# Five buffers and other rates for background loads, and recurrence levels two ahead, in a hybrid layer

## The chip, the cores and the metric

The kernel runs on one core of a Trainium2 chip. The metric is the device time of one execution in microseconds (us), as the median of several runs. PE is TensorE (matmul), PEld its weight load, DVE is VectorE, ACT is ScalarE, POOL is GpSimd, and SP is the queue that issues DMAs.

## The reference

One layer over 256 latent and 256 context tokens of width 2048, in float32: a modulation from the conditioning vector c, a normalization, one wide input projection that feeds differential attention (8 heads) and a gated linear recurrence in both directions (8 heads), a merge of both by sigmoid gates, an output projection, and a gated MLP with a convolution of width 3.

```python
mod = jax.nn.silu(c) @ w_mod[l] + b_mod[l]          # 2048 -> 6 * 2048
h = modulate(x, norm1_w, sh1, sc1)
ak, av, rff, rfb, ri, aq, rq, rg, gate_a, gate_r = split_cols(h @ w_in, len(IN_SPLITS))
a = p[:, :, 0] - lam * p[:, :, 1]                   # attention: two softmaxes a head
rec = rec_readout(o_f + o_b, rg, rec_gnorm_w)       # rms_norm(o) * silu(rg)
y = jax.nn.sigmoid(gate_a) * (att @ w_branch_attn) + jax.nn.sigmoid(gate_r) * (rec @ w_branch_rec)
x = x + g1 * (y @ w_out)
x = x + g2 * conv_ffn(modulate(x, norm2_w, sh2, sc2), w_up, conv_w, conv_b, w_down)
```

The first third of `mod` is needed at once. The other two thirds, 64 tiles of w_mod (g1, sh2, sc2, g2), are needed only behind the merge.

## The kernel before

**Weight units.** All weights come from HBM in units of 512 KB (128 x 1024, float32). `stage` issues the DMA of a unit on SP into `raw` (4 buffers, L68). ACT casts it to its high part `whi` (L72), DVE subtracts that to get the low part `wlo` (L73; 3 buffers each), and PE multiplies with both: in the three-pass `gemm` (L77 to L79, projections that need the context tokens too) 24 matmuls a unit, in `gemm2` (L136, L137) 16 matmuls, in pairs.

**Order.** A tile scheduler puts the instructions in an order of its own on every engine, from the program order, priorities (the cast and the subtraction of `stage` are raised) and the number of buffers behind each tag. After each unit the program calls `tick`, which may start a background unit and lets generators run on: the attention's `head` (scores with S at L432, the reduction at L435, exponentials at L439, transposes of the probabilities tp at L451) and the recurrence's `head` (KQ at L565, transposes tp and ktp at L597 and L604, products of levels lv at L629 that are copied into S at L632, the output op at L637 to L640). A `yield n` waits for n ticks.

**Stages.** Statistics and first modulation (to some 145 us), attention (to 418), recurrence (to 745), readout (the eight RG tiles, then the normalization rrstd at L712 and the products rec; to some 797), merge (16 tiles y, L743 to L769; to 1045), output projection, FFN.

**Background units.** The 64 late tiles of w_mod are computed on DVE in 128 units, first half 0 of all tiles, then half 1: a DMA of 512 KB (L382), and some ticks later (`age`) one multiplication with the broadcast SiLU of c, `cb[half]`, that also sums along the row (L93). `bg_rate` sets how many are started per tick. A unit that was loaded waits in `held`. In attention and merge the buffers are those of the tag x1 (4), of which the two halves `cb` hold two; in the recurrence the heads' outputs `rraw` hold the other two, and units use the weight units' own `raw` buffers. Ahead of the recurrence's heads, `background(max(0, len(bg) - 64))` starts in a burst what is left of half 0.

Of the kernel before, what the change touches and what calls it, by code (L numbers as in the profile page):

```python
# [8 lines left out]
F32 = mybir.dt.float32  # L9
F32R = mybir.dt.float32r  # L10
U32 = mybir.dt.uint32
AF = mybir.ActivationFunctionType
ALU = mybir.AluOpType
# [3 lines left out]
P = 128  # L17
D = 2048
T = 256
# [6 lines left out]
NB = 10  # L26
C1 = 3
BG_ATT0 = 0.5
BG_ATT, BG_REC, BG_MRG = 0.7, 0.1, 0.6
# [12 lines left out]
def body(ctx, tc, cst_d, sel_d, cb_d, ccol_d, wn_d, xT_d, xc_d, lam_d, rope_d, mask_d, wm_d, wg0_d, win_d, wba_d,  # L42
         wbr_d, wout_d, wu0_d, wup_d, wdn_d, out_d):
    nc = tc.nc
    act, dve, pool, pe, dma = nc.scalar, nc.vector, nc.gpsimd, nc.tensor, nc.sync

    cpool = ctx.enter_context(tc.tile_pool(name="cpool", bufs=1))
    stg = ctx.enter_context(tc.tile_pool(name="stg", bufs=1))
# [38 lines left out]
    held, age = [], [2]  # L87

    def background_end(least=0):

        while held and held[0][0] >= least:
            _, raw, c_, dst = held.pop(0)
            dve.scalar_tensor_tensor(raw, raw, 1.0, c_, op0=ALU.mult, op1=ALU.mult, accum_out=dst)  # L93
# [69 lines left out]
    xpair = [big.tile([P, 2, 512], F32, tag="x1", name=f"xp{i}", bufs=4) for i in range(4)]  # L163
# [3 lines left out]
    with ExitStack() as es:  # L167
# [156 lines left out]
        for i in range(7):  # L324
            r = big.tile([P, 512], F32, tag="ar", name=f"g0sb{i}", bufs=16)
            if i % 2:
                dve.tensor_copy(r, g0[i])
            else:
                act.copy(r, g0[i])
            g0raw[GROUP0[i]] = r  # L330

        cb = [big.tile([P, 1024], F32, tag="x1", name=f"cb{i}", bufs=4) for i in range(2)]
        sg = big.tile([P, 1024], F32, tag="x1", name="sg", bufs=4)
        for i in range(2):
            dma.dma_start(cb[i], cb_d[:, i * 1024:(i + 1) * 1024])
            tc.keep_in_program_order(act.activation(sg, cb[i], AF.Sigmoid))
            tc.keep_in_program_order(dve.tensor_mul(cb[i], cb[i], sg))
# [30 lines left out]
    with ExitStack() as esa:  # L368
        bg_rate[0] = BG_ATT


        lane = [True]

        def background(n):
            for _ in range(n):
                if bg:
                    t, half = bg.pop(0)
                    if lane[0]:
                        raw = big.tile([P, 1024], F32, tag="x1", name="bgraw", bufs=4)
                    else:  # L380
                        raw = stg.tile([P, 1024], F32, tag="raw", name="raw", bufs=4)
                    dma.dma_start(raw, wm_d[t - 32, half])  # L382
                    held.append([0, raw, cb[half], modp[:, t - 32, half:half + 1]])
# [4 lines left out]
        with ExitStack() as es:  # L388
# [6 lines left out]
            lj = at.tile([P, 64], F32, name="lj")  # L395
            lamt = at.tile([P, 256], F32, name="lamt")
            dma.dma_start(lamt, lam_d)
# [20 lines left out]
            def head(h, kT, vr, qT):  # L418
# [61 lines left out]
                rs = at.tile([P, 2, T], F32, tag="rs", name="rs")  # L480
                act.activation(rs[:, 0], ops[:, 1], AF.Sqrt, bias=epst, scale=1.0 / P)
                dve.reciprocal(rs[:, 1], rs[:, 0])
                dve.scalar_tensor_tensor(o, o, subw, rs[:, 1], op0=ALU.mult, op1=ALU.mult)
# [40 lines left out]
        lane[0], age[0] = False, 8  # L524
        rraw = [big.tile([P, 4, T], F32, tag="x1", name=f"rraw{i}", bufs=4) for i in range(2)]
        rrstd = cpool.tile([P, T], F32, name="rrstd")
        with ExitStack() as es:
# [29 lines left out]
            def head(h, kkq, kc, PL, PC, vr):  # L557
# [43 lines left out]
                yield 2 if h in (0, 1, 7) else 1  # L601
# [5 lines left out]
                E = level(0)  # L607
# [15 lines left out]

                for li in range(7):
                    En = level(li + 1) if li < 6 else None
                    yield 1
                    lvp = rps.tile([P, 2, P], F32, tag="lv", name="lv", bufs=3)
                    for m in range(2):
                        pe.matmul(lvp[:, m], E[:, 0, m * P:(m + 1) * P], E[:, 1, m * P:(m + 1) * P],  # L629
                                  start=True, stop=True)  # L630
                    for m in range(2):
                        dve.copy_predicated(out=S4[:, 3 * m], mask=masks[:, li].bitcast(U32), data=lvp[:, m])  # L632
                    E = En
# [18 lines left out]
            background(max(0, len(bg) - 64))  # L652
            background_end()
            g01 = big.tile([P, 2, 2, T], F32, tag="x1", name="g01", bufs=4)
            depth[0] = 1
            bg_rate[0] = BG_REC
            for h in range(8):
                PL, PC = PLs[h % 2], PCs[h % 2]
# [37 lines left out]

            rg8 = rt.tile([P, 9, T], F32, tag="f", name="rgs")
            rgs = [rg8[:, 4 * i:4 * i + 4] for i in range(2)]
            for h in range(8):
                ps = in_tile(RG + h)  # L700
                s = rgs[h // 4][:, h % 4]
                t_ = rt.tile([P, T], F32, tag="rg", name="rg")
                fold(t_, ps)
                act.activation(s, t_, AF.Sigmoid)
                pool.tensor_tensor(s, t_, s, ALU.mult)
# [24 lines left out]
    def residual_load(i):  # L730
        t_ = big.tile([P, 4, T], F32, tag="x1", name=f"x1_{i}", bufs=4)
        dma.dma_start(t_, xT_d[:, 4 * i:4 * i + 4])
        x1.append(t_)
# [6 lines left out]
    lane[0], age[0] = True, 3  # L740
    bg_rate[0] = BG_MRG
    y = []
    for j in range(KT):  # L743
        if j == 4:
            residual_load(0)
# [108 lines left out]
    for j in range(FT):  # L854
        cs = []
        for s in range(2):
# [19 lines left out]
            u = et.tile([P, T], F32, tag=f"u{s}", name="u", bufs=2)  # L876
# [136 lines left out]
```

## Time and profile before

| | |
|---|---|
| median of three runs | 1888.81 us |
| the three runs | 1888.81, 1885.11, 1890.86 us |
| profiled execution, its time | 1883.4 us |
| its span | 1881.6 us |
| mean granted clock of PE, share of full speed | 0.995 |

The profiled execution lasts 1.8 us longer than its span, and is within the spread of measurements a little shorter than the three runs. Busy shares are averages over stages of different kinds, so stretches are looked at one by one.

### The profile page before, as it was taken

How to read it: one execution, taken by the hardware profiler on the slowest of the kernel's cores; microseconds unless marked ns; L12 is line 12 of the kernel's file. 1: busy time of each engine (PE TensorE's matmuls, PEld its weight loads, DVE VectorE, ACT ScalarE, POOL GpSimd, SP SyncE). 2: the span in 40 equal slices, each digit the busy share in tenths (PEclk: the TensorE clock that was granted, in tenths of full speed). 3: DMA queues.
4: the chain of work that ended last, by engine and by line, in shares of the span. 5: the costliest groups of instructions: out<-in, count | busy, mean ns of one | idle time of the engine just before them, and what ended most of it. 6: DMA issues, size and time to landing. Idle time of an engine off the chain costs nothing.

```text
span 1881.6 us, 27926 instructions
## 1 busy us (share of the span) xinstructions
PE 1833.5 (97%) x10416; PEld 1558.2 (83%) x10416; DVE 1353.2 (72%) x2131; ACT 997.2 (53%) x1507; POOL 382.1 (20%) x328
## 2 busy tenths in 40 slices
PE   7999999999999999999999999999999999999997
PEld 4777777887788888888888889888888888888886
DVE  4449989779866667988886779776777677654444
ACT  4336444557655556744455557555555555534342
POOL 0002111103223333411111111222222222211111
PEclk9999999999999999999999999999999999999998
DMA  9977777474233333688997665666656666666664
GB/s 387 369 266 256 229 230 238 142 239 137 93 113 112 102 103 122 211 302 305 321 321 249 190 191 179 192 190 190 191 190 191 190 191 190 182 194 187 193 188 132
DMA packets 108711, 385.69 MB, mean 205 GB/s; under 512 B 12320, under 2 KB 12448, under 8 KB 108576
## 3 DMA queue, kind: packets, MB, share of 16 engines
q1 hardware_dynamic: 108576, 383.92, 63.1%
q8 instruction: 81, 1.33, 0.3%
q14 instruction: 54, 0.44, 0.1%
HBM read 381.78 MB, written 2.10 MB: 204 GB/s over the span
## 4 chain that ended last, share of the span: by engine, by line
PE 78%; DVE 11%; DMA 6%; issue 3%; ACT 2%; POOL 0%; SPq 0%; DVEq 0%; ACTq 0%; POOLq 0%
PE macc L136 30%; PE macc L137 15%; PE acc L136 6%; DMA bgraw<-in_wm 5%; PE acc L77 5%; PE acc L79 5%; PE acc L78 5%; DVE wlo L73 3%; PE acc L137 3%; PE g L187 2%; DVE bgraw L93 2%; PE acc L187 2%; PE nat L187 2%; PE lv L629 1%; ACT whi L72 1%
## 5 line engine op out<-in xcount | busy, mean ns | idle before, releaser
L73 DVE TENSOR_TENSOR wlo<-raw,whi 128x1024 fp32r<-128x1024 f32 (+1 forms) x514 | 628.6, 1224 | 240.0 <-ACT whi L72 234.7
L72 ACT CAST whi<-raw 128x1024 fp32r<-128x1024 f32 (+1 forms) x514 | 530.9, 1034 | 422.1 <-PE macc L136 159.2
L136 PE MATMUL macc<-h,whi 128*128 128x512 f32 x1344 | 466.0, 391 | 0.0
L137 PE MATMUL macc<-h,wlo 128*128 128x256 f32 x1344 | 376.3, 280 | 0.0
L136 PE MATMUL acc<-h,whi 128*128 128x512 f32 x896 | 320.9, 400 | 0.0
L136 PEld LDWEIGHTS macc<-h,whi 128*128 128x128 f32 x1344 | 251.3, 187 | 55.1
L137 PEld LDWEIGHTS macc<-h,wlo 128*128 128x128 f32 x1344 | 254.0, 189 | 0.0
L137 PE MATMUL acc<-h,wlo 128*128 128x256 f32 x896 | 252.5, 282 | 1.2 <-DVE wlo L73 1.0
L136 PE MATMUL macc<-f,whi 128*128 128x512 f32 x704 | 244.1, 391 | 0.0
L77 PE MATMUL acc<-h,whi 128*128 128x512 f32 x528 | 212.1, 402 | 0.0
L79 PE MATMUL acc<-h,wlo 128*128 128x512 f32 x528 | 207.3, 393 | 0.3 <-DVE wlo L73 0.3
L78 PE MATMUL acc<-h,whi 128*128 128x512 f32 x528 | 206.4, 391 | 0.0
L136 PEld LDWEIGHTS acc<-h,whi 128*128 128x128 f32 x896 | 168.4, 188 | 37.7 <-issue 0.4
L137 PE MATMUL macc<-f,wlo 128*128 128x256 f32 x704 | 197.1, 280 | 0.0
L137 PEld LDWEIGHTS acc<-h,wlo 128*128 128x128 f32 x896 | 169.3, 189 | 4.9 <-DVE wlo L73 4.3
L93 DVE SCALAR_TENSOR_TENSOR bgraw<-bgraw,cb 128x1024 f32<-128x1024 f32 x105 | 133.0, 1268 | 36.8 <-DMA bgraw<-in_wm 36.0
L136 PEld LDWEIGHTS macc<-f,whi 128*128 128x128 f32 x704 | 131.6, 187 | 28.9
L884 POOL TENSOR_TENSOR u<-u 128x256 f32<-128x256 f32 x44 | 69.2, 1572 | 326.5 <-DVE u L879 286.5
L137 PEld LDWEIGHTS macc<-f,wlo 128*128 128x128 f32 x704 | 133.1, 189 | 0.0
L77 PEld LDWEIGHTS acc<-h,whi 128*128 128x128 f32 x528 | 99.2, 188 | 22.8 <-issue 4.3
L79 PEld LDWEIGHTS acc<-h,wlo 128*128 128x128 f32 x528 | 99.1, 188 | 22.6 <-DVE wlo L73 0.8
L78 PEld LDWEIGHTS acc<-h,whi 128*128 128x128 f32 x528 | 99.3, 188 | 19.2 <-issue 0.4
(752 smaller groups left out, 2674.4 us busy)
## 6 DMA issues: line engine op xcount, KB each, us to landing
raw<-in_win SPq DMA_DIRECT2D x178, 512.0 KB, 4.3
raw<-in_wup SPq DMA_DIRECT2D x168, 512.0 KB, 3.6
bgraw<-in_wm SPq DMA_DIRECT2D x105, 512.0 KB, 4.7
raw<-in_wdn SPq DMA_DIRECT2D x80, 512.0 KB, 3.6
nraw<-in_wn SPq DMA_DIRECT2D x64, 512.0 KB, 7.5
raw<-in_wout SPq DMA_DIRECT2D x32, 512.0 KB, 3.5
raw<-in_wm SPq DMA_DIRECT2D x23, 512.0 KB, 3.6
raw<-in_wba SPq DMA_DIRECT2D x16, 512.0 KB, 4.7
```

Of the source, the lines that this page charges most:

```text
L72: act.copy(hi[:, :n], raw[:, :n])
L73: dve.tensor_sub(lo[:, :n], raw[:, :n], hi[:, :n].bitcast(F32))
L77: pe.matmul(ps, wh, xh, start=first, stop=False)
L78: pe.matmul(ps, wh, xl, start=False, stop=False)
L79: pe.matmul(ps, wl, xh, start=False, stop=last)
L93: dve.scalar_tensor_tensor(raw, raw, 1.0, c_, op0=ALU.mult, op1=ALU.mult, accum_out=dst)
L136: pe.matmul(ps, hi[:, c_], xs[k][:, :, :T], start=k == 0, stop=False)
L137: pe.matmul(ps[:, :T], lo[:, c_], xs[k][:, 0, :T], start=False, stop=k == len(xs) - 1)
L187: tc.keep_in_program_order(pe.matmul(*args, **kw))
L629: pe.matmul(lvp[:, m], E[:, 0, m * P:(m + 1) * P], E[:, 1, m * P:(m + 1) * P], start=True, stop=True)
L884: pool.tensor_tensor(cs[1], cs[0], cs[1], ALU.mult)
```

## The change

There are five x1 buffers for four (one natural-layout buffer fewer, NB, and small tiles that share tags). Only half 0 of `cb` is prepared ahead of the attention; half 1 is loaded and multiplied by its sigmoid just before the readout. A unit of half 1 can't start before that. Rates and ages are new in all three stages: .5/.7 to .55/.77 in the attention, .1 to .05 in the recurrence, .6 to .74 in the merge; ages 2, 8 and 3 become 4, 3 and 5. The burst moves from ahead of the recurrence's heads to behind them, and all units use x1 buffers. In the recurrence's heads, head 0 and head 1 wait one and two ticks longer ahead of ktp, and levels E are made two ahead of their use instead of one. The residual's first load comes two tiles of y later, and the FFN's two tiles u become one.

```diff
-NB = 10
+NB = 9
-BG_ATT0 = 0.5
-BG_ATT, BG_REC, BG_MRG = 0.7, 0.1, 0.6
+BG_ATT0 = 0.55
+BG_ATT, BG_REC, BG_MRG = 0.77, 0.05, 0.74
+AGE_ATT, AGE_REC, AGE_MRG = 4, 3, 5
...
-    xpair = [big.tile([P, 2, 512], F32, tag="x1", name=f"xp{i}", bufs=4) for i in range(4)]
+    xpair = [big.tile([P, 2, 512], F32, tag="x1", name=f"xp{i}", bufs=5) for i in range(4)]
...
-        cb = [big.tile([P, 1024], F32, tag="x1", name=f"cb{i}", bufs=4) for i in range(2)]
-        sg = big.tile([P, 1024], F32, tag="x1", name="sg", bufs=4)
-        for i in range(2):
-            dma.dma_start(cb[i], cb_d[:, i * 1024:(i + 1) * 1024])
-            tc.keep_in_program_order(act.activation(sg, cb[i], AF.Sigmoid))
-            tc.keep_in_program_order(dve.tensor_mul(cb[i], cb[i], sg))
+        cb = {}
+
+        def cond(half, sg):
+
+            part = cb[half] = big.tile([P, 1024], F32, tag="x1", name=f"cb{half}", bufs=5)
+            dma.dma_start(part, cb_d[:, half * 1024:(half + 1) * 1024])
+
+            def rest():
+                tc.keep_in_program_order(act.activation(sg, part, AF.Sigmoid))
+                tc.keep_in_program_order(dve.tensor_mul(part, part, sg))
+            return rest
+
+        cond(0, big.tile([P, 1024], F32, tag="x1", name="sg", bufs=5))()
...
-                    t, half = bg.pop(0)
-                    if lane[0]:
-                        raw = big.tile([P, 1024], F32, tag="x1", name="bgraw", bufs=4)
-                    else:
-                        raw = stg.tile([P, 1024], F32, tag="raw", name="raw", bufs=4)
+                    t, half = bg[0]
+                    if half not in cb:
+                        return
+                    bg.pop(0)
+                    raw = big.tile([P, 1024], F32, tag="x1", name="bgraw", bufs=5)
                     dma.dma_start(raw, wm_d[t - 32, half])
-                    held.append([0, raw, cb[half], modp[:, t - 32, half:half + 1]])
+                    held.append([0, operation(raw, t, half)])
...
-        lane[0], age[0] = False, 8
-        rraw = [big.tile([P, 4, T], F32, tag="x1", name=f"rraw{i}", bufs=4) for i in range(2)]
+        age[0] = AGE_REC
+        rraw = []
...
-                yield 2 if h in (0, 1, 7) else 1
+                yield {0: 3, 1: 4, 7: 2}.get(h, 1)
...
-                E = level(0)
+                Es = [level(0)]
...
+                Es.append(level(1))
                 for li in range(7):
-                    En = level(li + 1) if li < 6 else None
+                    if li < 5:
+                        Es.append(level(li + 2))
                     yield 1
+                    E = Es.pop(0)
...
-                    E = En
...
-            background(max(0, len(bg) - 64))
-            background_end()
...
             for h in range(8):
+                if h % 4 == 0:
+                    rraw.append(big.tile([P, 4, T], F32, tag="x1", name=f"rraw{h}", bufs=5))
...
+            background(max(0, len(bg) - 64))
+            background_end()
+            held.append([0, cond(1, stg.tile([P, 1024], F32, tag="raw", name="sg", bufs=4))])
+
             rg8 = rt.tile([P, 9, T], F32, tag="f", name="rgs")
...
-    lane[0], age[0] = True, 3
+    age[0] = AGE_MRG
...
-        if j == 4:
+        if j == 6:
             residual_load(0)
...
+        us = et.tile([P, 2, T], F32, tag="gate", name="u", bufs=3)
...
-            u = et.tile([P, T], F32, tag=f"u{s}", name="u", bufs=2)
+            u = us[:, s]
```

How the change moves instructions is seen in the order of each engine, at three places.

On DVE, in the attention, in front of the eleventh reduction of scores (L435 before, L442 after); rows with modp are background operations (L93 before, L378 after). Before:

```order
L153 TENSOR_TENSOR qr<-qr,acc 128x256
L93 SCALAR_TENSOR_TENSOR bgraw,modp<-bgraw,cb_1243 128x1024
L412 STREAM_SHUFFLE rot<-qr 128x256
L93 SCALAR_TENSOR_TENSOR bgraw,modp<-bgraw,cb_1243 128x1024
L73 TENSOR_TENSOR wlo<-raw,whi 128x1024
L416 TENSOR_TENSOR qr<-t_2663,rot 128x256
L93 SCALAR_TENSOR_TENSOR bgraw,modp<-bgraw,cb_1243 128x1024
L514 TENSOR_TENSOR qT<-qr,qT 128x256
L93 SCALAR_TENSOR_TENSOR bgraw,modp<-bgraw,cb_1243 128x1024 x2
L73 TENSOR_TENSOR wlo<-raw,whi 128x1024
L482 RECIPROCAL rs<-rs 128x256
L435 TENSOR_REDUCE z<-S 128x2
```

and with the change:

```order
L461 TENSOR_TENSOR aT<-tp,aT 128x4x128
L153 TENSOR_TENSOR qr<-qr,acc 128x256
L378 SCALAR_TENSOR_TENSOR bgraw,modp<-bgraw,cb_1244 128x1024
L419 STREAM_SHUFFLE rot<-qr 128x256
L378 SCALAR_TENSOR_TENSOR bgraw,modp<-bgraw,cb_1244 128x1024
L423 TENSOR_TENSOR qr<-t_2667,rot 128x256
L74 TENSOR_TENSOR wlo<-raw,whi 128x1024
L521 TENSOR_TENSOR qT<-qr,qT 128x256
L378 SCALAR_TENSOR_TENSOR bgraw,modp<-bgraw,cb_1244 128x1024 x5
L74 TENSOR_TENSOR wlo<-raw,whi 128x1024
L489 RECIPROCAL rs<-rs 128x256
L442 TENSOR_REDUCE z<-S 128x2
```

Five background operations stood in the rows in front of the reduction, now there are seven, five of them in a row. Two subtractions wlo, on which PE's next units depend, stand among them in both orders.

On DVE, in the readout, around KQ of the last recurrence head (L565 before, L572 after); L716 and L729 are the readout's products. Before:

```order
L591 TENSOR_TENSOR E<-E,kkq 128x2x128
L93 SCALAR_TENSOR_TENSOR raw,modp<-raw,cb_1244 128x1024
L716 SCALAR_TENSOR_TENSOR rgs<-rraw_3599,cst,rgs 128x256
L73 TENSOR_TENSOR wlo<-raw,whi 128x1024 x2
L565 TENSOR_TENSOR KQ<-KQ,kc 128x512
L153 TENSOR_TENSOR rg<-rg,acc 128x256
L73 TENSOR_TENSOR wlo<-raw,whi 128x1024
L716 SCALAR_TENSOR_TENSOR rgs<-rraw_3599,cst,rgs 128x256
L586 TENSOR_TENSOR E<-PL_3625 128x256
L73 TENSOR_TENSOR wlo<-raw,whi 128x1024
```

and with the change:

```order
L729 SCALAR_TENSOR_TENSOR rgs<-rraw_3641,cst,rgs 128x256
L74 TENSOR_TENSOR wlo<-raw,whi 128x1024
L153 TENSOR_TENSOR rg<-rg,acc 128x256
L378 SCALAR_TENSOR_TENSOR bgraw,modp<-bgraw,cb_6360 128x1024
L74 TENSOR_TENSOR wlo<-raw,whi 128x1024
L729 SCALAR_TENSOR_TENSOR rgs<-rraw_3641,cst,rgs 128x256
L572 TENSOR_TENSOR KQ<-KQ,kc 128x512
L378 SCALAR_TENSOR_TENSOR bgraw,modp<-bgraw,cb_6360 128x1024
L74 TENSOR_TENSOR wlo<-raw,whi 128x1024 x2
L378 SCALAR_TENSOR_TENSOR bgraw,modp<-bgraw,cb_6360 128x1024
L593 TENSOR_TENSOR E<-PL_3636 128x256
L74 TENSOR_TENSOR wlo<-raw,whi 128x1024
```

One background operation stood there; now there are three, each between subtractions.

On PE, at the start of the recurrence, in front of the transposes ktp of head 1 (the names h with a number are the input's tiles, h_219 the first and h_1185 the last). Before:

```order
L77 MATMUL acc<-h_1185,whi 128x512
L78 MATMUL acc<-h_1185,whi 128x512
L79 MATMUL acc<-h_1185,wlo 128x512
L604 MATMUL ktp<-ident,KQ 128x128 x4
L610 MATMUL dc<-E 128x128
L611 MATMUL dc<-E 128x128
L613 MATMUL dc<-kkq,ksum 128x128 x2
```

and with the change:

```order
L78 MATMUL acc<-h_668,whi 128x512
L79 MATMUL acc<-h_668,whi 128x512
L80 MATMUL acc<-h_668,wlo 128x512
L611 MATMUL ktp<-ident,KQ 128x128 x4
L617 MATMUL dc<-E 128x128
L618 MATMUL dc<-E 128x128
L620 MATMUL dc<-kkq,ksum 128x128 x2
```

Between head 1's tp and ktp there was one three-pass unit, the second half of a tile (24 weight matmuls); now there are two units of `gemm2` and one three-pass unit, the first half of a tile (56).

## Rows read from the trace of the kernel before

**Rows 1.** The page's first part: span, and busy time, share and instructions of each engine.

```profile
span 1881.6 us, 27926 instructions
PE 1833.5 (97%) x10416; PEld 1558.2 (83%) x10416; DVE 1353.2 (72%) x2131; ACT 997.2 (53%) x1507; POOL 382.1 (20%) x328
```

**Rows 2.** The page's chain that ended last, by engine.

```profile
PE 78%; DVE 11%; DMA 6%; issue 3%; ACT 2%; POOL 0%; SPq 0%; DVEq 0%; ACTq 0%; POOLq 0%
```

**Rows 3.** Stretches: length, busy us of PE, PEld, DVE, ACT, POOL; clock, DMA, GB/s.

```profile
150.00:320.00 170.00, 160.51 (x804) 128.00 (x803) 152.82 (x262) 82.34 (x147) 28.32 (x23) 1.00 0.72 236
425.00:500.00 75.00, 68.15 (x360) 56.94 (x359) 65.85 (x112) 55.61 (x78) 27.42 (x25) 0.98 0.38 120
500.00:740.00 240.00, 240.00 (x1240) 205.01 (x1239) 168.02 (x327) 133.04 (x181) 74.06 (x72) 1.00 0.34 106
740.00:800.00 60.00, 58.22 (x345) 50.97 (x345) 57.16 (x99) 48.21 (x73) 25.30 (x22) 1.00 0.65 202
800.00:1005.00 205.00, 202.21 (x1136) 173.07 (x1136) 175.40 (x258) 98.75 (x155) 27.64 (x25) 1.00 0.89 314
1005.00:1130.00 125.00, 125.00 (x723) 110.24 (x722) 91.86 (x130) 67.55 (x112) 19.87 (x19) 1.00 0.63 193
1160.00:1860.00 700.00, 700.00 (x4040) 617.18 (x4040) 449.07 (x604) 376.10 (x545) 164.23 (x117) 1.00 0.63 189
```

**Rows 4.** Waits of PE in the whole span: us in total, times, longest.

```profile
PE S L432 <- ACT p L439: 7.8, 6, 2.6
PE tp L451 <- DVE p L445: 3.0, 4, 1.6
```

**Rows 5.** Waits of DVE from 150 to 320 us.

```profile
DVE bgraw L93 <- DMA bgraw<-in_wm: 12.0, 10, 2.3
```

**Rows 6.** Stretches of one attention head each, the same columns.

```profile
242.70:277.90 35.20, 33.60 (x171) 27.09 (x170) 30.50 (x53) 16.37 (x30) 5.26 (x4) 1.00 0.74 241
349.00:382.10 33.10, 33.04 (x169) 26.83 (x168) 22.17 (x38) 16.70 (x30) 2.99 (x4) 1.00 0.36 112
```

**Rows 7.** The tile bgraw from 800 to 1005 us: durations, and times to landing.

```profile
L93 DVE SCALAR_TENSOR_TENSOR bgraw<-bgraw,cb x50: 1210/1226/1761, 799.4 to 993.1; 128x1024 f32<-128x1024 f32 x50
DMA to landing us min/median/max: 3.4/5.3/7.2
```

**Rows 8.** Waits of PE from 425 to 500 us.

```profile
PE ktp L604 <- DVE KQ L565: 2.8, 1, 2.8
PE lv L629 <- ACT E L588: 1.7, 1, 1.7
PE lv L629 <- DVE E L591: 1.0, 2, 0.6
```

**Rows 9.** Timeline of DVE in the readout: start, duration, line, operation.

```profile
775.54 0.50 DVE L632 COPY_PREDICATED S<-masks,lv 128x128 f32<-128x128 uint32 x2
775.93 0.42 DVE L590 TENSOR_TENSOR E<-E,kkq 128x256 f32<-128x256 f32 x1
776.27 0.42 DVE L591 TENSOR_TENSOR E<-E,kkq 128x256 f32<-128x256 f32 x1
776.61 1.22 DVE L73 TENSOR_TENSOR wlo<-raw,whi 128x1024 fp32r<-128x1024 f32 x1
777.74 0.41 DVE L153 TENSOR_TENSOR rg<-rg,acc 128x256 f32<-128x256 f32 x1
```

**Rows 10.** Timeline of ACT in the readout.

```profile
745.26 1.28 ACT L704 ACT_TABLE_LOAD   x1
746.56 0.42 ACT L704 ACTIVATE rgs<-rg 128x256 f32<-128x256 f32 x1
```

**Rows 11.** Waits of DVE from 800 to 1005 us.

```profile
DVE bgraw L93 <- DMA bgraw<-in_wm: 23.7, 29, 2.1
```

**Rows 12.** Waits of SP's DMA queue from 800 to 1005 us.

```profile
SPq L382 <- DVE bgraw L93: 21.3, 13, 2.9
```

**Rows 13.** Waits of PE in the whole span, the natural-layout tiles.

```profile
PE nat L187 <- DMA nraw<-in_wn: 0.6, 1, 0.6
```

More of the change, by code (lines that the diff above doesn't have):

```diff
@@ L86, in body @@
     bgf = [None]
-    held, age = [], [2]
+    held, age = [], [AGE_ATT]
     def background_end(least=0):
         while held and held[0][0] >= least:
-            _, raw, c_, dst = held.pop(0)
-            dve.scalar_tensor_tensor(raw, raw, 1.0, c_, op0=ALU.mult, op1=ALU.mult, accum_out=dst)
+            held.pop(0)[1]()
     def tick(n):
@@ L369, in body, with operation @@
         bg_rate[0] = BG_ATT
-        lane = [True]
+        def operation(raw, t, half):
+            return lambda: dve.scalar_tensor_tensor(raw, raw, 1.0, cb[half], op0=ALU.mult, op1=ALU.mult,
+                                                    accum_out=modp[:, t - 32, half:half + 1])
         def background(n):
@@ L394, in body @@
             ls = at.tile([P, 6], F32, name="ls")
-            lj = at.tile([P, 64], F32, name="lj")
-            lamt = at.tile([P, 256], F32, name="lamt")
-            dma.dma_start(lamt, lam_d)
+            lamt = big.tile([P, 320], F32, tag="ar", name="lamt", bufs=16)
+            lj = lamt[:, 256:]
+            dma.dma_start(lamt[:, :256], lam_d)
             for i in range(2):
@@ L479, in head @@
                 pe.matmul(ops[:, 1], ones, osq, start=True, stop=True)
[L480 to L483, printed above, removed]
+                rs = at.tile([P, T], F32, tag="rs", name="rs")
+                act.activation(rs, ops[:, 1], AF.Sqrt, bias=epst, scale=1.0 / P)
+                dve.reciprocal(rs, rs)
+                dve.scalar_tensor_tensor(o, o, subw, rs, op0=ALU.mult, op1=ALU.mult)
                 a = big.tile([P, 2, T], F32R, tag="ar", name=f"att{h}", bufs=16)
@@ L650, in head @@
                     pool.tensor_tensor(sqacc, sqacc, sq, ALU.add)
-            background(max(0, len(bg) - 64))
-            background_end()
-            g01 = big.tile([P, 2, 2, T], F32, tag="x1", name="g01", bufs=4)
+            g01 = big.tile([P, 2, 2, T], F32, tag="x1", name="g01", bufs=5)
             depth[0] = 1
@@ L701, in body @@
                 s = rgs[h // 4][:, h % 4]
-                t_ = rt.tile([P, T], F32, tag="rg", name="rg")
+                t_ = rt.tile([P, T], F32, tag="sq", name="rg")
                 fold(t_, ps)
@@ L730, in residual_load @@
     def residual_load(i):
-        t_ = big.tile([P, 4, T], F32, tag="x1", name=f"x1_{i}", bufs=4)
+        t_ = big.tile([P, 4, T], F32, tag="x1", name=f"x1_{i}", bufs=5)
         dma.dma_start(t_, xT_d[:, 4 * i:4 * i + 4])
```

## The prediction

> **What bounds the kernel now.** I read the page first. TensorE (PE) is busy for 97% of the span [rows 1], and the chain that ended last runs over PE for 78%, over VectorE (DVE) for 11% and over DMA for 6% [rows 2]. So an edit earns something only in a stretch where PE is not full, and costs something only where it makes PE wait. The table by stretches shows where that is [rows 3]. From 500 to 740 us (recurrence) and from 1160 us on, PE is busy for the whole stretch. It is short by 9.5 us in 150 to 320 (attention), 6.9 us in 425 to 500 (start of the recurrence) and 1.8 us in 740 to 800 (readout).
>
> The merge (800 to 1005) looks nearly full, but its matmuls are spread out. In the stretch behind it, with the same kind of matmul, 723 of them take 125 us, 0.173 us each. At that pace the merge's 1136 would take 196.4 us, and they have 205, so 8.6 us are lost there. Altogether some 27 us are to be had, in four places.
>
> **Attention, 150 to 320 us.** What is late there: PE waits for the softmax's exponentials and for the scaled probabilities [rows 4], and both come behind DVE. DVE is busy for 152.8 of 170 us [rows 3], and 12.0 of its 17.2 idle us are waits of background operations for their own DMA [rows 5]. A head's period is 35.2 us where the units run at the full rate, with PE busy for 33.6; in the last head, where DVE is busy for only 22.2 us, the period is 33.1 [rows 6]. A head thus loses 2.1 us.
>
> The change works both ways here. Four buffers instead of two let a load start earlier, so the 12.0 us can go. But by the order, 53 instead of 43 background operations stand between the first and the eleventh REDUCE. At 1.22 us each (median of a unit, [rows 7]) that is 12.2 us more. Busy 165.0 plus the 5.2 us of other idle time gives 170.2 us for a stretch of 170: what the buffers give, the rate takes. The burst ahead of the eleventh REDUCE grows from five operations to seven, 2.4 us on the chain to the scores. I take +2. The lower end is -4 (a little under half of the 9.5 us comes back, if the waits go early and the added operations fall in gaps). The upper end is +12 (no wait goes, and all added operations are on the path). Behind the eleventh REDUCE 2 units stand instead of 19, but PE already runs at its own pace there (33.0 of 33.1, [rows 6]), so this relief is worth nothing.
>
> **Start of the recurrence.** PE waits 2.8 us at head 1's ktp for KQ, and 1.7 and 1.0 us for levels E [rows 8]. The change takes away the burst in front of the heads, and puts 56 instead of 24 weight matmuls between head 1's tp and ktp. The 32 added ones are worth 5.5 us at 0.173 us, more than the 2.8 us wait, unless KQ itself slips. Levels made two ahead should take about half of the other 2.7 us. That makes 2.8 + 1.4 = 4.2, so -4. Bounds: -6.9 (all that PE lacks there) and 0 (KQ comes later by as much). In the rest of the recurrence PE is full, with nothing to win; the 4 units fewer there free time on an engine that has 72 us idle already [rows 3].
>
> **Readout, 740 to 800 us.** This is the place where the change pays. DVE is busy for 57.2 of 60 us and PE for 58.2 [rows 3], so DVE has 2.8 us to spare. Between head 7's scans and the reciprocal of rrstd, the order has on DVE 10 background operations instead of 4, 28 copies into S instead of 19, 31 operations on E instead of 24, 18 wlo instead of 16, and the product for the second half of the conditioning vector. From start to next start [rows 9], a copy takes 0.20 us (0.39 for two), an operation on E 0.34, a wlo 1.13. So the addition is 6 x 1.22 = 7.3, 9 x 0.2 = 1.8, 7 x 0.34 = 2.4, 2 x 1.13 = 2.3, and the product at most a wlo, 1.2: together 15.0 us. PE gets its own share: two units (32 matmuls, 5.5 us) and nine level matmuls (1.5), 7.0 us. The other 8.0, less the 2.8 us idle, make PE wait: +5. The lower end is 0, if the three wlo buffers that PE may have ahead cover it. The upper end is +11: no idle time is of use, and each of the six added units costs the longest of such operations, 1.76 us [rows 7], which is 3.2 more.
>
> ScalarE (ACT) gets about five more table loads here, since sigmoids and exponentials alternate. One takes 1.28 us, and the sigmoid behind it starts 1.30 us after its start [rows 10], so nothing lies between them. ACT then has 48.2 busy us, 6.4 of loads, some 2 of casts for the two units and 2 of exponentials and sigmoid: 59 in a stretch of about 67, so I let it cost nothing. The Trainium skill, "ScalarE: Activation LUTs", section What ACT_TABLE_LOAD costs, adds about 1380 ns of drain to each load's 1283 ns. This trace agrees with the load and shows no drain before the sigmoid. By the page ACT would get an estimated 6.9 us more, about 66 of 67, and the readout's term would lie nearer to its upper end.
>
> **Merge, 800 to 1005 us.** DVE waits 23.7 us, in 29 waits, for a unit's DMA [rows 11]; a transfer lands after 5.3 us [rows 7]. A third buffer lets the loads go that are held for a buffer: 21.3 us, but in 13 waits out of 48 loads [rows 12]. The others are issued right behind weight loads, and in the order of both kernels the operation stands two wlo units behind its load. Two units are 32 matmuls, 5.5 us, hardly more than the landing time. So the longer age doesn't move the operation away from its load, and most waits stay. About a quarter of 8.6 us (13 of 48) is 2.3. By the order all 128 units are done at y11 before, and six of them come behind y11 now, closer to the sums that need them, so I take -1.5. Bounds: -8.6 (all that is lost) and +2 (the six units, 7.3 us of DVE, of which a quarter makes PE wait).
>
> **At nothing:** one buffer fewer in the first stage (PE waits once, 0.6 us, for such a load, [rows 13]); the second half's load and sigmoid, which no longer stand in front of the attention; the FFN's u in one tile (PE full behind 1160 us, [rows 3]); the residual's load two tiles later, whose data are read only after the merge; shared small tiles. If the first stage's cover is gone, it is +1.
>
> **Sum:** +2 - 4 + 5 - 1.5 = +1.5 on the profiled execution's 1883.4 us (span 1881.6). That execution is 5.4 us under the median of the three runs, 1888.8, so the forecast is 1890. A measurement of this kernel can tell about 0.3% (5.7 us) from no change, so this is "same".
>
> **Rivals.** (A) Faster: the buffers do end the waits for DMA. In the attention -4, at the recurrence's start -4, in the merge -6 of the 8.6, in the readout +5: -9, 1880 us. For it speaks the order of the attention, where the distance from load to use grows from 1.3 to 2.6 wlo units over the first thirty units; against it the unchanged distance in the merge. It decides if the merge's 29 waits fall under ten. The Trainium skill, "Perfetto Trace Analysis", section Optimization Strategy, says that the same gap repeating on the engine that should be saturated can mean too little memory for the next tile; the lost 2.1 us in a head and the merge's spread matmuls are such gaps. Chance 0.28. (B) Slower: the readout costs its upper end, since DVE has no time to spare and each S copy, E and unit queues ahead of a wlo: +11 + 2 - 4 - 1.5 = +7.5, 1896 us. It decides when DVE is full there and PE waits over 8 us for wlo, S or rec. Chance 0.18. (C) Slower: the attention's DVE runs full and the scores are late by the whole 12.2 us: +12 - 4 + 5 - 1.5 = +11.5, 1900 us. For it speaks DVE's 90%, against it that the last heads have no units left. Chance 0.12. (D) The change does nothing that PE notices, as 97% suggests: 1889 us. Chance 0.12. My forecast: 0.30.
>
> **How the numbers follow.** Forecast and (D) are within 0.3%: 0.42. (A) is faster: 0.28. (B) and (C) are slower: 0.30. The range goes from a little under (A), 1878, to (C) with some of (B), 1903. The likeliest case's own range is 1885 to 1895.
>
> **What would show it.** In the new profile: in 150 to 320 us about 56 background operations, no longer waits for DMA over 4 us, and PE still short by about 10 us; no wait at ktp over 0.5 us; the stretch from head 7's scans to the reciprocal of rrstd 10 to 13 us longer on DVE, and DVE without a gap in it; more table loads there; in the merge some 20 waits for DMA. I am wrong if the merge's matmuls run at 0.173 us (then A), or if PE's waits for the scores double (then C).

## The result, and the profile after

The changed kernel takes 1913.9 us (median of 4 runs, 1911.1 to 1916.4), the kernel before 1888.7 us: a ratio of 1.0137, with a 95% interval of 1.0121 to 1.0153. It is 25 us slower, and the forecast was 1890 with a range of 1878 to 1903.

The page of the changed kernel, first part and chain:

```profile
span 1914.5 us, 27877 instructions
PE 1846.1 (96%) x10416; PEld 1568.2 (82%) x10416; DVE 1360.2 (71%) x2131; ACT 1006.1 (53%) x1514; POOL 386.9 (20%) x328
...
PE 71%; DVE 12%; DMA 6%; ACT 4%; issue 4%; POOL 1%; SPq 0%; DVEq 0%; ACTq 0%; POOLq 0%
```

Against [rows 1] and [rows 2], PE is busy for 12.6 us more and idle for 20.3 us more; its share of the chain fell from 78% to 71%. Stretches of the changed kernel, with the columns of [rows 3]:

```profile
150.00:320.00 170.00, 162.65 (x817) 130.47 (x816) 165.84 (x288) 80.46 (x145) 30.95 (x23) 1.00 0.80 269
425.00:500.00 75.00, 71.44 (x379) 59.99 (x378) 62.67 (x105) 55.62 (x73) 25.20 (x21) 1.00 0.40 131
500.00:740.00 240.00, 222.70 (x1094) 188.87 (x1093) 154.60 (x285) 122.16 (x169) 68.04 (x66) 0.96 0.29 90
1160.00:1860.00 700.00, 700.00 (x4096) 620.26 (x4095) 463.13 (x637) 381.69 (x560) 158.38 (x112) 1.00 0.63 189
```

The loss is in the stretch from 500 to 740 us. There PE was busy for all 240 us before; now it is busy for 222.7, and its granted clock is 0.96, a mean over stretches at 2.4 GHz and others at 1.2 GHz. From 1160 us on nothing has changed. PE's waits in the whole span, with the attention's beside (compare [rows 4]):

```profile
PE lv L639 <- DVE E L598: 18.3, 7, 4.7
PE S L439 <- ACT p L446: 8.9, 7, 3.2
...
PE acc L136 <- DVE rg L153: 3.3, 2, 2.2
```

The first row did not exist at this size: seven waits for a level's E, up to 4.7 us. From 500 to 740 us, where the kernel before had no wait of PE, there are five, one in each of heads 1 to 5:

```profile
PE lv L639 <- DVE E L598: 15.1, 4, 4.7
PE lv L639 <- DVE S L642: 2.1, 1, 2.1
```

To see where time goes, the start of the same subtraction wlo on DVE was compared between profiles of the kernels (the k-th of 530, so that the same weights are meant). Difference to the kernel before, in us, one profile each (the columns are the changed kernel; the kernel before with the new waits ahead of ktp; the changed kernel with the old waits; with old waits and levels one ahead; and with E and the copies into S raised in priority, all told below):

```
place (us in before)         changed  before+waits  waits old  waits, levels old  E and S raised
start of attention (144.6)     +1.1      +2.6         -0.5         -0.3             +1.3
end of attention (416.6)       +0.4      +1.5         -1.6         -1.3             +0.4
early recurrence (466.7)       -0.3      +1.0         -1.9         -1.6             -1.7
end of recurrence (744.5)     +24.9     +19.6         +2.1         +2.1             -0.4
readout (785.0)               +30.0     +24.7         +6.4         +6.4            +12.4
behind the merge (1063.2)     +33.4     +26.3         +9.4         +7.7             +9.0
```

Between early recurrence and its end the changed kernel loses 25.2 us. Single profiles differ too: the kernel before with another tag for the readout's tile, whose orders on PE and DVE are the same as before up to the readout, stood at +3.2 at the end of the attention. So differences of some 3 us in this table say nothing. The profiled execution of before was some 5 us under its median, so at the end all kernels look some us later than their medians do.

One such wait, at 614 us. On DVE (start, duration, line, operation):

```profile
607.21 0.43 DVE L597 TENSOR_TENSOR E<-E,kkq 128x256 f32<-128x256 f32 x1 [0.72 <-ACT E L595]
607.55 1.77 DVE L692 TENSOR_TENSOR_SCAN PL<-ones,fq 128x256 f32<-128x256 f32 x2
609.24 1.69 DVE L74 TENSOR_TENSOR wlo<-raw,whi 128x1024 fp32r<-128x1024 f32 x1
610.86 1.10 DVE L692 TENSOR_TENSOR_SCAN PL<-ones,fq 128x256 f32<-128x256 f32 x1
611.88 1.62 DVE L694 TENSOR_TENSOR_SCAN PC<-ones,fq 128x256 f32<-128x256 f32 x2
613.42 0.47 DVE L642 COPY_PREDICATED S<-masks,lv 128x128 f32<-128x128 uint32 x2
613.80 0.42 DVE L598 TENSOR_TENSOR E<-E,kkq 128x256 f32<-128x256 f32 x1
```

and on PE at the same time:

```profile
610.05 0.39 PE L80 MATMUL acc<-h,wlo 128*128 128x512 f32 x1
610.27 0.60 PE L639 MATMUL lv<-E 128*128 128x128 f32 x4
614.36 0.68 PE L639 MATMUL lv<-E 128*128 128x128 f32 x4 [3.48 <-DVE E L598]
...
616.23 0.63 PE L80 MATMUL acc<-h,wlo 128*128 128x512 f32 x1
```

A level's first product (L597) is made at 607.2, its second one (L598) at 613.8. Between them stand the five scans of the next head (L692, L694) and a wlo, 5.9 us (607.55 to 613.42) in which DVE does nothing for the running head's levels, and two copies into S. PE has gone through a unit's weight matmuls at 610.3, multiplies one level, and waits 3.48 us for the next. In the kernel before, the same block of scans meets a head that has its level products behind it. The last one stands on PE at 602.9 us and waits for nothing, and only copies into S follow:

```profile
600.88 1.84 DVE L683 TENSOR_TENSOR_SCAN PL<-ones,fq 128x256 f32<-128x256 f32 x3
602.65 1.25 DVE L685 TENSOR_TENSOR_SCAN PC<-ones,fq 128x256 f32<-128x256 f32 x2
603.81 0.67 DVE L632 COPY_PREDICATED S<-masks,lv 128x128 f32<-128x128 uint32 x3
...
602.92 0.60 PE L629 MATMUL lv<-E 128*128 128x128 f32 x4
```

In the changed kernel, matmuls of the same form behind the wait take 0.63 us for 0.39 (616.23 and 610.05). Windows around it, with the columns of [rows 3]:

```profile
596.00:610.00 14.00, 14.00 (x75) 12.06 (x74) 10.04 (x15) 12.22 (x14) 7.02 (x7) 1.00 0.13 41
610.80:614.30 3.50, 0.08 (x1) 0.00 (x0) 3.50 (x8) 1.56 (x2) 1.57 (x2) 1.00 0.49 150
614.80:619.20 4.40, 4.40 (x15) 3.46 (x14) 4.40 (x14) 1.26 (x2) 0.00 (x0) 0.61 0.11 7
619.20:630.00 10.80, 10.80 (x55) 9.09 (x54) 3.77 (x11) 2.58 (x3) 0.00 (x0) 1.00 0.25 96
...
561.90:568.00 6.10, 6.10 (x17) 4.94 (x18) 5.47 (x17) 1.26 (x2) 0.00 (x0) 0.50 0.20 50
```

The granted clock is 1.00 ahead of the wait, 0.61 for 4.4 us behind it, that is mostly at 1.2 GHz, and 1.00 again. So this wait costs 1.7 us more (0.39 x 4.4). The price is not the same for each: behind the wait in head 2, which ends at 561.8 us and lasts 3.49 us too, the clock is 0.50 for 6.1 us (last row), some 3 us lost, and behind the last one, of 2.15 us up to 715.5 us, it is 1.00 (715.5 to 725 us). In the whole stretch, 17.3 us of idle time and an estimated 0.04 x 240 = 9.6 us of clock make 26.9, a little more than the loss of 25.2 between the two places of the table.

The edits that the prediction counted as terms show as follows. DVE's waits for DMA in the attention, 150 to 320 us ([rows 5]):

```profile
DVE bgraw L378 <- DMA bgraw<-in_wm: 2.3, 1, 2.3
```

and in the merge, from 830 to 1035 us because of the delay ([rows 11]):

```profile
DVE bgraw L378 <- DMA bgraw<-in_wm: 26.1, 26, 3.3
```

The background operations in the attention, 57 of them (shortest, median and longest in ns):

```profile
L378 DVE SCALAR_TENSOR_TENSOR bgraw<-bgraw,cb x57: 1194/1214/1758, 153.0 to 315.0; 128x1024 f32<-128x1024 f32 x57
```

### The profile page after: what moved, and what is told of

Read it like the earlier page. It is cut to its first block, busy times and chain, and to the rows that moved or that the text cites. A ratio compares the mean times of both kernels' runs of the same rounds, so it can differ in the third digit from the quotient of the medians.

```text
span 1914.5 us, 27877 instructions
## 1 busy us (share of the span) xinstructions
PE 1846.1 (96%) x10416; PEld 1568.2 (82%) x10416; DVE 1360.2 (71%) x2131; ACT 1006.1 (53%) x1514; POOL 386.9 (20%) x328
## 4 chain that ended last, share of the span: by engine, by line
PE 71%; DVE 12%; DMA 6%; ACT 4%; issue 4%; POOL 1%; SPq 0%; DVEq 0%; ACTq 0%; POOLq 0%
PE macc L136 29%; PE macc L137 15%; DMA bgraw<-in_wm 5%; PE acc L136 5%; DVE wlo L74 4%; PE acc L78 3%; PE acc L79 3%; PE acc L80 3%; PE acc L137 3%; PE g L187 2%; PE acc L187 2%; DVE bgraw L378 2%; PE nat L187 2%; ACT whi L73 1%; PE lv L639 1%
## 5 line engine op out<-in xcount | busy, mean ns | idle before, releaser
L136 PE MATMUL acc<-h,whi 128*128 128x512 f32 x896 | 323.4, 402 | 3.3 <-DVE rg L153 3.3
L78 PE MATMUL acc<-h,whi 128*128 128x512 f32 x528 | 215.3, 408 | 0.0
L79 PE MATMUL acc<-h,whi 128*128 128x512 f32 x528 | 209.8, 397 | 0.0
L136 PEld LDWEIGHTS acc<-h,whi 128*128 128x128 f32 x896 | 169.2, 189 | 41.8 <-DVE rg L153 3.7
L378 DVE SCALAR_TENSOR_TENSOR bgraw<-bgraw,cb 128x1024 f32<-128x1024 f32 x128 | 159.9, 1257 | 32.5 <-DMA bgraw<-in_wm 32.1
L78 PEld LDWEIGHTS acc<-h,whi 128*128 128x128 f32 x528 | 101.6, 193 | 24.0 <-issue 4.7
L79 PEld LDWEIGHTS acc<-h,whi 128*128 128x128 f32 x528 | 101.3, 192 | 19.5 <-issue 0.4
```

Of the source, the lines that this page charges most:

```text
L78: pe.matmul(ps, wh, xh, start=first, stop=False)
L79: pe.matmul(ps, wh, xl, start=False, stop=False)
L136: pe.matmul(ps, hi[:, c_], xs[k][:, :, :T], start=k == 0, stop=False)
L378: return lambda: dve.scalar_tensor_tensor(raw, raw, 1.0, cb[half], op0=ALU.mult, op1=ALU.mult, accum_out=modp[:, t - 32, half:half + 1])
```

## The experiments

All of them are kernels with a part of the change undone or done alone, or with the level chain raised in priority. They separate three explanations. **P**: the longer waits ahead of ktp shift all later heads against the weight units. **L**: the levels made two ahead. **S** against **B**, for the readout: a shared small tile, against background work. **Q** was set up after the first runs: the block of scans on DVE holds back whatever of the level chain stands behind it, and the place of the level products on PE doesn't matter.

**The waits ahead of ktp, set back.**

```diff
-                yield {0: 3, 1: 4, 7: 2}.get(h, 1)
+                yield 2 if h in (0, 1, 7) else 1
```

> The changed kernel with the waits ahead of ktp set back (2, 2, 1, ..., 1, 2), levels still two ahead. Theory P (the three ticks that heads 0 and 1 wait longer shift every later head against the next head's scans, and PE then waits for E at a pair of level products): the five waits of 2.2 to 4.7 us in 500 to 740 us go, the clock there is back at 1.00, and the readout loses its nine late copies into S; about 1886 us. Theory L (the levels made two ahead put the later E behind the scans): the waits stay, about 1912 us.

Measured: 1894.3 us, ratio 1.0030 [1.0017, 1.0044]. Twenty of the 25 us are gone.

```profile
500.00:740.00 240.00, 237.44 (x1225) 202.62 (x1224) 163.63 (x314) 134.13 (x182) 72.37 (x72) 1.00 0.31 97
```

PE is busy for 237.4 of 240 us, and the clock is back. P holds, L falls. The readout keeps its loss, contrary to the expectation: +4.3 us there in the table, with the waits of before.

**The levels, one ahead.**

```diff
-                Es.append(level(1))
                 for li in range(7):
-                    if li < 5:
-                        Es.append(level(li + 2))
+                    if li < 6:
+                        Es.append(level(li + 1))
```

> The changed kernel with levels one ahead, the new waits ahead of ktp kept. Theory P: the waits at the level products stay, or grow, since E is made later still: 1912 us or more. Theory L: they go, about 1888 us.

Measured: 1906.8 us, 1.0102 [1.0085, 1.0119]. The waits stay (18.0 us for E, ten times). Yet levels two ahead cost some 7 us at the new waits, which neither theory said; what makes up this difference was not isolated.

**Both set back.** The two edits above together.

> The changed kernel with both set back, so that only buffers, rates, ages, the late second half and the moved burst are left. Either theory: the recurrence's loss of some 24 us is gone. If the rest is worth what the prediction's sum said without these parts, about 1890; if the merge's +2 and the readout's part seen in the changed kernel's trace remain, about 1892; under 1885 if these parts earn something once the recurrence doesn't hide it.

Measured: 1893.3 us, 1.0024 [1.0008, 1.0039]. What is left of the change (buffers, rates, ages, late second half, moved burst, shared tiles) costs 4.7 us, nearest to the second value of the expectation.

**The waits alone, in the kernel before.**

```diff
-                yield 2 if h in (0, 1, 7) else 1
+                yield {0: 3, 1: 4, 7: 2}.get(h, 1)
```

> The kernel before with the new waits ahead of ktp alone. Theory P: it gets the waits at the level products in every head and a later end of head 7, about 1910 us, with levels one ahead perhaps more. Theory L: about 1889 us.

Measured: 1912.1 us, 1.0131 [1.0108, 1.0153]. One line of the change makes nearly all of its loss:

```profile
500.00:740.00 240.00, 224.40 (x1117) 190.85 (x1118) 159.90 (x299) 124.69 (x170) 71.96 (x69) 0.97 0.31 95
```

PE's waits for E in this stretch:

```profile
PE lv L629 <- DVE E L591: 16.2, 6, 3.4
```

**Levels two ahead alone, in the kernel before.**

```diff
-                    En = level(li + 1) if li < 6 else None
+                    if li < 5:
+                        Es.append(level(li + 2))
```

> The kernel before with levels two ahead alone. Theory P: nothing changes, since no later head waits for a level: 1888 to 1891 us. Theory L: 1895 us or more.

Measured: 1888.6 us, 0.9993 [0.9979, 1.0007]: nothing, as P said.

**Other shifts.** In the kernel before, only the numbers of ticks are changed, an early kernel and one with a shift of one tick:

```diff
-                yield 2 if h in (0, 1, 7) else 1
+                yield {0: 2, 1: 4, 2: 0, 3: 0, 7: 2}.get(h, 1)
```

```diff
-                yield 2 if h in (0, 1, 7) else 1
+                yield {0: 2, 1: 3, 7: 2}.get(h, 1)
```

> The kernel before with the longer wait ahead of head 1's ktp (4 ticks), given back in heads 2 and 3 (0 ticks), so that the later heads run ahead of their old place: by the order 97 copies into S stand ahead of head 7's scans, 93 before and 84 in the changed kernel. Theory P: no wait at the level products in heads 3 to 6, the wait for KQ of 2.8 us gone, 1885 to 1888 us. If the longer wait itself cost the time, not the phase: 1895 us or more.

> The kernel before with 3 ticks ahead of head 1's ktp instead of 2: a shift by one tick, with 88 copies into S ahead of head 7's scans (93 before, 84 in the changed kernel). Theory P, if the cost grows with the shift: some 8 to 12 us, about 1899 us. If only the full shift collides with the scans: about 1888 us.

Measured: 1896.3 us, 1.0037 [1.0020, 1.0054], for the early one; 1906.1 us, 1.0089 [1.0060, 1.0118], for the shift of one tick, more than either value of its expectation. PE's waits for the copies into S from 500 to 740 us, in the early kernel:

```profile
PE lv L629 <- DVE S L632: 4.0, 1, 4.0
```

and with the shift of one tick:

```profile
PE lv L629 <- DVE S L632: 10.6, 6, 2.3
```

By the order, the copies into S that the running head still has to make behind head 7's first scan are 1 in the early kernel, 5 in the kernel before, 10 with one tick, and 14 in the changed kernel: with the last three the loss grows, 0, 16 and 25 us (of the changed kernel, with all its other edits). The early kernel missed its expectation, and is 6 us slower than before; by its time alone it falls to the other case, in which the longer wait itself costs the time. (That case is answered further down, by a run that keeps the longer waits and loses little.) PE has one wait of 4.0 us in this stretch, in head 1, which is not yet at the early place, and none in the later heads; that and the clock behind it may be most of the 6 us, but no run isolates it.

**The readout's small tile.** In the kernel before, one edit:

```diff
-                t_ = rt.tile([P, T], F32, tag="rg", name="rg")
+                t_ = rt.tile([P, T], F32, tag="sq", name="rg")
```

> The kernel before with one edit: the readout's tile rg takes the tag sq, which it then shares with ksum and the squares of the heads. Theory S (the shared buffer holds the folds back until head 7's ksum has been read, PE waits for an accumulator, and head 7's chain ends later): some 18 us between the first and the second fold instead of 9, the readout 3 to 4.5 us longer, about 1892 us. Theory B (the readout's loss comes from background work and the second half of the conditioning vector): 1888.6 us, no change.

Measured: 1896.8 us, 1.0035 [1.0020, 1.0050]. The folds of the first two RG tiles on DVE's timeline, for the kernel before:

```profile
745.63 0.42 DVE L153 TENSOR_TENSOR rg<-rg,acc 128x256 f32<-128x256 f32 x1
754.43 0.41 DVE L153 TENSOR_TENSOR rg<-rg,acc 128x256 f32<-128x256 f32 x1
```

for this one:

```profile
750.25 0.41 DVE L153 TENSOR_TENSOR rg<-rg,acc 128x256 f32<-128x256 f32 x1
765.97 0.41 DVE L153 TENSOR_TENSOR rg<-rg,acc 128x256 f32<-128x256 f32 x1
```

and for the changed kernel with waits and levels set back:

```profile
746.30 0.42 DVE L153 TENSOR_TENSOR rg<-rg,acc 128x256 f32<-128x256 f32 x1
764.74 0.41 DVE L153 TENSOR_TENSOR rg<-rg,acc 128x256 f32<-128x256 f32 x1
```

Between them lie 8.8, 15.7 and 18.4 us. The buffer of the tag sq holds ksum of head 7, so the second RG tile can't be folded until ksum has been read (in the changed kernel it is the fourth: folds at 783.8 and 802.1 us). PE then waits for an accumulator, 1.1 us in this run and 3.3 us in the changed kernel (the third of PE's rows above). S holds for the held fold and for the time, beyond B's "no change"; but the accumulator's wait is a small part of the 6.8 us, and which waits make up the rest was not isolated.

**That tile in another buffer.** The changed kernel with waits and levels set back, and rg in the buffer of kc:

```diff
-                t_ = rt.tile([P, T], F32, tag="sq", name="rg")
+                t_ = rt.tile([P, 2, T], F32, tag="kc", name="rg")[:, 0]
```

> The changed kernel with waits and levels set back, and rg in the buffer of kc, which is free when KQ of head 7 has been made. Theory S: the folds come earlier and the readout's loss of 4.3 us shrinks to 1 or less: about 1889 us. Theory B: it stays at about 1893 us.

Measured: 1891.4 us, 1.0008 [0.9995, 1.0021]. With the tile moved too, nothing measurable is left of the rest of the change. That was not 1889, but within the interval of no change, so of B at most about 4 us is left. The interval overlaps that of the run with the tile shared, and in the profile the readout still loses 3.0 us, for 4.3; so this run doesn't show by itself what the tile costs in the changed kernel.

**E ahead of the scans.** In the changed kernel, exponential and products of a level raised:

```diff
+                    with tc.high_priority(offset=200):
                         act.activation(E, E, AF.Exp)
...
```

> The changed kernel with the new waits and levels two ahead, and the exponential and the products of each level raised in priority by 200, so that both products of a level stand ahead of the next head's scans on DVE. Theory P in its narrow form (PE waits because the second product of a pair of levels stands behind the five scans): the waits of 3.5 to 4.7 us go, the clock from 500 to 740 us is back near 1.00, some 15 to 20 us of the 25 come back, about 1895 to 1899 us. If the shifted place itself is the cause, whatever stands ahead of the scans: 1910 us or more.

Measured: 1911.1 us, 1.0114 [1.0088, 1.0140]. The narrow form fell; by its time this run goes with the other case, the shifted place itself. The rows say otherwise. PE's waits from 500 to 740 us:

```profile
PE lv L640 <- DVE S L643: 14.8, 4, 5.3
PE lv L640 <- DVE E L599: 3.3, 1, 3.3
```

and DVE's timeline at the scans of one head:

```profile
607.20 0.43 DVE L598 TENSOR_TENSOR E<-E,kkq 128x256 f32<-128x256 f32 x1 [0.92 <-ACT E L596]
607.54 0.42 DVE L599 TENSOR_TENSOR E<-E,kkq 128x256 f32<-128x256 f32 x1
607.87 1.27 DVE L693 TENSOR_TENSOR_SCAN PL<-ones,fq 128x256 f32<-128x256 f32 x2
609.05 1.25 DVE L695 TENSOR_TENSOR_SCAN PC<-ones,fq 128x256 f32<-128x256 f32 x2
610.22 0.67 DVE L643 COPY_PREDICATED S<-masks,lv 128x128 f32<-128x128 uint32 x3
```

Both products now stand ahead of the last four scans (607.2 and 607.5), as intended. But three copies into S (L643, 610.22) stand behind them, and PE now waits for these: an accumulator lv (three buffers) is free again only when its copy is made. One wait took the place of the other.

**Differences raised as well, with the tile moved.** Beside the tile's edit:

```diff
...
+                    with tc.high_priority(offset=200):
                         eng = pool if li in (3, 5) else dve
                         eng.tensor_tensor(Ev[:, :, :, 0], rl, Lv, ALU.subtract)
                         eng.tensor_tensor(Ev[:, :, :, 1], Rv, rr, ALU.subtract)
...
```

> The changed kernel with the differences, exponentials and products of the levels all raised by 200, and rg in the buffer of kc. Theories P and S together: no wait for E above 1 us, the readout without the held folds, the wait for KQ gone as in the changed kernel; 1885 to 1892 us. If the late end of head 7 costs by itself: 1893 to 1898 us.

Measured: 1900.4 us, 1.0060 [1.0039, 1.0082].

```profile
500.00:740.00 240.00, 231.42 (x1187) 197.30 (x1188) 159.11 (x307) 128.41 (x179) 76.56 (x75) 1.00 0.30 95
```

PE's waits for the copies in this stretch:

```profile
PE lv L641 <- DVE S L644: 6.8, 5, 2.0
```

The waits for the copies are 1.2 to 2.0 us now, and the clock from 500 to 740 us is 1.00: behind these shorter waits no lowered clock is seen. Two theories together, but not the whole: 1900.4 us is above both ranges of the expectation.

**The same with levels one ahead.** The levels' edit from above is added.

> As h2, with levels one ahead. If levels two ahead cost some 7 us at the new waits because more of E stands behind the scans, raising E takes that away, and this comes out with h2 within 2 us. If levels one ahead leave E too late even when raised: 4 us or more slower than h2.

Measured: 1917.1 us, 1.0145 [1.0117, 1.0173], 17 us slower than with levels two ahead: the second case of the expectation. The profiled execution was the slowest of the five, 1928.9 us. In it PE waits 2.8 us for E in head 1 and 2.8 to 3.3 us for the copies in each of the four heads behind it, and the clock is 0.96 again. That E made only one level ahead comes too late is what the expectation said; the waits for the copies don't show it, and the cause was not isolated.

**E and copies raised.** The changed kernel with exponential, products, differences and copies raised:

```diff
...
+                    with tc.high_priority(offset=200):
+                        for m in range(2):
+                            dve.copy_predicated(out=S4[:, 3 * m], mask=masks[:, li].bitcast(U32), data=lvp[:, m])
```

> The changed kernel with all of a level raised by 200, the copies into S too. Theory Q (one block of some 6 us on DVE, the next head's five scans and a wlo, holds back whatever of the level chain stands behind it, first the second product of E, then the copy that frees the level's accumulator): no wait over 1 us at the level products in heads 1 to 6, the clock at 1.00, the recurrence within 4 us of the kernel before, and about 1897 us with what the readout still loses. If it is the place of the level products on PE itself: waits over 1 us stay, 1905 us or more.

Measured: 1893.4 us, 1.0023 [1.0013, 1.0033]; 20.5 us under the changed kernel, although the new waits ahead of ktp are kept.

```profile
500.00:740.00 240.00, 239.45 (x1233) 204.96 (x1234) 164.88 (x319) 134.30 (x184) 77.06 (x76) 0.99 0.31 97
```

The only wait of PE at a level there:

```profile
PE lv L641 <- DVE E L600: 3.8, 1, 3.8
```

PE is busy for 239.5 of 240 us, with the level products at the shifted place: in heads 2 to 5 the same numbers of weight matmuls stand ahead of each level product as in the changed kernel (1856 ahead of head 2's first one, 1792 in the kernel before). One wait is left, 3.8 us in head 1. Q holds: it is DVE's order at the scans, not the place on PE, nor the longer waits themselves. Part of the gain is lost again in the readout, where this kernel's profile loses 12.8 us (12.4 + 0.4 in the table), for 5.1 in the changed kernel; why was not isolated.

**And the tile moved.** The same, with rg in the buffer of kc.

> The same with rg in the buffer of kc. Theories Q and S together: 3 to 5 us less than the run without it, about 1893 us, some 3 us over the kernel before for the later end of head 7; if the later end costs nothing, 1889 us.

Measured: 1889.7 us, 1.0011 [0.9996, 1.0026]. The changed kernel with these two mendings is level with the kernel before. No version that was run beats it by more than can be measured.

## Why the prediction was wrong

**The step that failed: "In the rest of the recurrence PE is full, with nothing to win".** I put the waits ahead of ktp down to the start of the recurrence, as a gain of 2.8 us there, and took the rest at zero because PE had no idle time there. Full is a reason for no gain; it is none for no loss. The heads run one behind the other and did not make the three ticks up: by the order 37, 51, 65, 79 and 93 copies into S stood ahead of the scans of heads 3 to 7, and 28, 42, 56, 70 and 84 in the changed kernel, nine fewer each time. So every later head's level products met the next head's five scans. By P and Q, that cost 19.6 us in the changed kernel (1913.9 to 1894.3), and 23.6 alone. I had seen the sign of it, nine copies more behind head 7's scans, and booked it to the readout only. The prediction also costed no wait that PE could get behind the scans, and nothing for the clock, an estimated 9.6 us here. A sign of the clock's price stood in [rows 3], where the stretch from 425 to 500 us has 0.98: in the kernel before, it is at half right behind the wait of 2.8 us for KQ.

```profile
482.20:485.60 3.40, 3.33 (x14) 3.02 (x15) 3.30 (x9) 2.39 (x5) 0.00 (x0) 0.50 0.11 7
```

**Start of the recurrence, -4.** The wait for KQ is gone, as said; the waits for E at head 0 stayed at 1.7 and 1.0 us, so the half of them that levels two ahead should have taken did not come. Before a gain could show, head 1's first wait of 4.7 us stood there.

**Attention, +2.** The mechanism was right. 57 background operations stand there (46 before, 56 forecast), DVE is busy for 165.8 of 170 us (165.0 forecast), waits for DMA fell from 12.0 to 2.3 us, and PE waits 8.9 us for the exponentials as before (7.8). The cost is -0.7 us (0.4 - 1.1), within a profile's uncertainty, so that nothing was won or lost. That the buffers gave what the rate took is the forecast's argument; no run sets buffers, ages and rates apart.

**Readout, +5.** The profiles give +5.1 in the changed kernel (30.0 - 24.9) and +4.3 with the waits of before (6.4 - 2.1). But the cause I gave, DVE's additional work, was at most a part: DVE was to be without a gap, and it is busy for 52.3 of the 60 us from 768 to 828. One term of PE's share was too small besides: the two products of a level take 0.60 us (610.27 above), so nine products take 2.7 us, not 1.5. Where I put "shared small tiles" at nothing, the shared rg alone costs 6.8 us in the kernel before (3.8 to 9.4), and two of the runs with it moved come out some 3 to 4 us lower (1893.3 to 1891.4, with the kernel before at 1888.6 and 1890.0; and 1893.4 to 1889.7), though their intervals overlap. That the number came out was luck. Rival (B) had the right place, but not its condition: from 765 to 840 us PE waits 3.3 us for the accumulator and 5.4 us at level products, and not for wlo, S or rec.

**Merge, -1.5.** 26 waits for DMA with 26.1 us stand there, 29 with 23.7 before; "most waits stay" was right, and the gain did not come: +3.4 us in the profile (33.4 - 30.0), +1.3 with waits and levels set back (7.7 - 6.4), within what profiles differ by. SP's waits for a unit's own buffer fell from 21.3 us [rows 12] to 2.3, and DVE's waits for the transfer did not fall. By the order the operation stands as close to its load as before; that this is the reason is argued, not tested.

**Rivals.** (A)'s condition failed: 26 waits are not under ten. The Trainium skill's rule, "Perfetto Trace Analysis", section Optimization Strategy, on gaps from too little memory, agrees with the attention's waits for DMA, which fell from 12.0 to 2.3 us with the added buffers and the longer ages, not told apart here; PE's own gaps there mostly stayed (7.4 us of 9.5). (C) foresaw DVE full in the attention, and it was full, without the cost. None of them named the shift.

**Open:** why levels two ahead cost 7 us at the new waits; what the early kernel loses; what makes up the readout's loss; and how the last 1 to 3 us of the rest of the change divide.

## What to carry to other kernels

When work of two pipelined heads is interleaved by counts, a delay in one head is a shift of all that follow: look, by the order, at what each engine does next to the shifted work in the steady state, not only where the delay is put. A full engine in the profile means that nothing is to be won there; time can still be lost. A tile that takes another's tag gets its lifetime as well, so sharing is free only if the other's last reader is early; and a wait removed from one instruction behind a block comes back at the next one behind it, until all that the consumer needs stands in front.

## What the runs showed of the hardware that was not expected

TensorE's granted clock fell at the end of, or behind, four of the changed kernel's five waits from 500 to 740 us: 0.61 over the 4.4 us after one of 3.48 us, 0.50 over 6.1 us after one of 3.49 us, and 0.96 over the 240 us. It was 1.00 over the same stretch in the run with five waits of 1.2 to 2.0 us and one of 2.7. The length of a wait alone doesn't decide it: with the shift of one tick, a wait of 2.25 us at 614.0 us was followed by 1.00 (614 to 618 us), one of 2.24 us at 663.5 us by 0.50 (663.7 to 667.1 us). The lower level is 1.2 GHz; the matmuls there took 0.63 us for 0.39. By the windows the clock cost over a third of this loss, and no idle time shows it.
